# Longer bursts in a gated recurrence, and two gate products on split operands, in a two-layer hybrid attention trunk

## The chip, the cores and the metric

The kernel runs on one core of a Trainium2 chip. A core has a matrix engine (TensorE, "PE" in the profile, with its weight loads as "PEld"), a vector engine (VectorE, "DVE"), a scalar engine (ScalarE, "ACT"), GpSimd ("POOL") and a queue engine that issues the DMAs ("SP"). Matrix results land in PSUM, of which this kernel uses eight banks of 128 x 512 float32; everything else is in SBUF. The metric is the device time of one execution in microseconds (us); lower is better. Three runs of the kernel before took 2611.86, 2612.74 and 2614.28 us.

## What is computed

Two layers over 2048 tokens of width 1024. Each layer normalises and modulates its input, projects it, and sends the result through two branches: four heads of gated linear attention (GLA), and four heads of differential softmax attention. The change touches the GLA branch and one line on the way into the softmax branch. The reference, cut to the GLA branch:

```python
log_a = jax.nn.log_sigmoid((glr @ w_gk + b_gk)) / 16.0        # glr: tokens x 16, w_gk: 16 x 256
log_a = log_a.reshape(B, nc, 64, 4, 64)                       # chunks of 64 tokens, 4 heads, 64 wide
b = jnp.cumsum(log_a, axis=2)
b_end = b[:, :, -1]
k_dec = k * jnp.exp(b_end[:, :, None] - b)
u = jnp.einsum('bnchk,bnchv->nbhkv', k_dec, v)                # one 64 x 128 update a chunk and head
a = jnp.exp(b_end)
state = a_c[..., None] * state + u_c                          # scan over the 32 chunks
o = jnp.einsum('bnchk,nbhkv->bnchv', q, states)               # the chunk reads the state at its end
o = rms_norm(o, g_out) * silu(z)
```

## The kernel before

The sequence is cut into four units of 512 tokens (`u`), each of four tiles of 128 tokens (`t`), each of two chunks of 64. With two layers there are eight units. All large products are made of parts: an operand is split into a high part, rounded to the type `float32r`, and the low remainder, and three `float32r` products stand for one float32 product. Smaller products run on plain float32 operands; the trace shows such a matmul as two matmul instructions, a `float32r` one as a single one.

**What sets the order.** The program is first recorded, not issued. Six generators (projections, softmax heads, GLA, preparation of the next unit, modulation, query and key transposes) are interleaved by `run_streams` with their own estimates (`pe(cost, wait)`). The recorded operations then go through `Program.order` (lines 199 to 296), a list scheduler with a table of costs, latencies and free buffers, which fixes the sequence of each engine's queue. On the chip every engine works through its queue in that order and waits at the head of it. `prog.together` (line 160) makes a run of matmuls stay one burst on TensorE. All instructions are issued from line 305, so the profile's groups are told apart by the names of their tiles.

**The stages that the change touches.** In `gla_gen` (line 717), once a unit:

- The low-rank gate: 16 `float32r` matmuls of `wglr` with the input's high and low parts give `gps`, 32 rows of 512 tokens (16 rows for the weight's high part, 16 for its low part). VectorE copies them to `gT`, whose row 32 is set to 1.
- The gate's second product (line 742): four float32 matmuls, one for each tile of 128 tokens, of `gT` (33 rows) with `wgk` (33 rows x 256: the weight twice, and the bias). ScalarE and VectorE make the log-sigmoid `la` from it.
- The chunk sums (line 757): four float32 matmuls with the triangular matrix `tri`, 128 x 256 each; their exponential is `E`. Line 762 makes the chunks' totals from `la` and `chk`, 32 columns wide, in four column strips side by side (`a_sb` after a transpose).
- The recurrence (lines 805 to 849), for each tile of 128 tokens: a burst of 8 matmuls of 64 x 64 x 128 (`sc<-vN,E`) into two PSUM banks; four VectorE instructions that carry the state `Sn` over two chunks; a burst of 8 matmuls `po<-Sn,qT` into two other banks; the norm of the result: ScalarE squares (`sq`), VectorE sums (`gss`), GpSimd takes the power -1/2 (`gw`), VectorE multiplies into `osb` (shown under the tile's name `vN`).

The four PSUM banks of the tag `tp` serve these bursts and all of the gate's products, and also the softmax heads' scores (`sc`), transposes (`tp`) and outputs (`po`); the other four banks (`acc`) hold the large projections.

In `head_evac` (line 867), a softmax head's projection leaves PSUM: ScalarE copies queries and keys to `rw`, and VectorE writes the normalised ones to another tile, `qk`, which TensorE transposes later (`qk_gen`, line 892). `gate_weights` (line 444) loads `wgk` and splits the weight of the low-rank product into `wglr`; it runs in the start phase for layer 0 and during layer 0 for layer 1.

## Time and profile before

| | |
|---|---|
| runs, median of 3 | 2612.74 us (2611.86 to 2614.28) |
| the profiled execution | 2617.78 us, of which its span is 2616.0 us |
| granted TensorE clock, mean | 0.993 |
| DVE busy | 1758.4 us (67%) |
| ACT busy | 1202.3 us (46%) |
| POOL busy | 616.0 us (24%) |
| DMA | 476.12 MB, mean 182 GB/s |

The span runs from the first to the last instruction of one execution; the profiled execution was 5.04 us above the median of the runs. "Busy" is the time in which at least one instruction of the engine was in flight. Matmuls overlap: the next starts while the last still drains, so the mean duration of one (some 400 ns for 512 columns) is longer than the distance from one start to the next (some 230 ns), and it is the distance that costs time. In a timeline row, instructions that follow each other are merged with their count; its second column runs to the end of the last of them.

### The profile page before, as it was taken

What the parts mean: (1) busy time and instruction counts of PE and PEld (TensorE: products, weight loads), DVE (VectorE), ACT (ScalarE), POOL (GpSimd) and SP (SyncE); (2) the same over time, 40 slices, a digit from 0 to 9 for tenths busy, and PEclk for the clock granted to TensorE, in tenths of its full rate; (3) what the DMA queues carried; (4) which work ended last, traced back from release to release, by engine and by line L of the source; (5) the groups of instructions that cost most, each with busy time, mean ns of one, the idle gap of its engine ahead of it and who ended that gap; (6) DMA issues with size and microseconds to landing.
All of it is one profiled execution on the core that took longest, in us unless ns stands there. A gap on an engine that the chain in (4) does not pass through costs nothing. (4 is left out here: it accounts for less than half of the span.)

```text
span 2616.0 us, 40988 instructions
## 1 busy us (share of the span) xinstructions
PE 2513.0 (96%) x13987; PEld 2041.7 (78%) x13987; DVE 1758.4 (67%) x5072; ACT 1202.3 (46%) x2592; POOL 616.0 (24%) x820
## 2 busy tenths in 40 slices
PE   7999899999999999999999999999999999999997
PEld 4776677777888778888777777887788877888886
DVE  4778757874667846677748784657737786387864
ACT  3555523453354543544634564344614556154543
POOL 2445511122010210101144554111211111210111
PEclk9999999999999999999999999999999999999998
DMA  8777686555553455444267767554474443734342
GB/s 279 239 236 251 203 300 195 159 175 195 187 176 120 154 181 195 133 141 143 88 237 251 247 211 252 170 177 148 135 262 155 150 149 102 264 122 150 107 149 89
DMA packets 201612, 476.12 MB, mean 182 GB/s; under 512 B 20734, under 2 KB 78268, under 8 KB 201404
## 3 DMA queue, kind: packets, MB, share of 16 engines
q1 hardware_dynamic: 201404, 473.50, 54.2%
q8 instruction: 111, 1.82, 0.3%
q14 instruction: 97, 0.79, 0.1%
HBM read 362.29 MB, written 111.15 MB: 181 GB/s over the span
## 5 line engine op out<-in xcount | busy, mean ns | idle before, releaser
L305 PE MATMUL acc<-w,hhi 128*128 128x512 f32 x2560 | 838.9, 402 | 7.0 <-ACT ub L305 2.6
L305 PEld LDWEIGHTS acc<-w,hhi 128*128 128x128 f32 x2560 | 464.9, 189 | 100.5 <-ACT ub L305 7.7
L305 PE MATMUL acc<-w,hlo 128*128 128x512 f32 x1280 | 505.4, 396 | 0.0
L305 ACT ACTIVATE s<-s,mx 128x512 f32<-128x512 f32 (+15 forms) x256 | 308.1, 1204 | 351.0 <-DVE s L305 349.6
L305 PE MATMUL acc<-hhi,w 128*128 128x512 f32 x1024 | 370.7, 403 | 1.4 <-DVE z L305 1.2
L305 PE MATMUL acc<-w,oh 128*128 128x512 f32 x1024 | 330.8, 401 | 11.5 <-DVE t L305 7.1
L305 DVE TENSOR_SCALAR_CACHE_REDUCE s<-sc,mx 64x64 f32<-64x64 f32 (+5 forms) x640 | 307.1, 485 | 36.3 <-PE sc L305 19.1
L305 POOL MEMSET s<- 64x64 f32 x256 | 39.4, 156 | 1074.4 <-DVE s L305 527.1
L305 PEld LDWEIGHTS acc<-w,hlo 128*128 128x128 f32 x1280 | 241.4, 189 | 48.7 <-issue 1.3
L305 POOL TENSOR_TENSOR w<-raw,w 128x512 fp32r<-128x512 f32 x144 | 196.1, 1371 | 191.4 <-ACT w L305 158.9
L305 PEld LDWEIGHTS acc<-w,oh 128*128 128x128 f32 x1024 | 189.7, 190 | 58.4 <-DVE t L305 14.3
L305 PEld LDWEIGHTS acc<-hhi,w 128*128 128x128 f32 x1024 | 192.3, 188 | 39.2 <-PE tp L305 1.9
L305 PE MATMUL po<-Vj,aT 128*128 128x128 f32 x1536 | 206.1, 278 | 8.6 <-ACT aT L305 8.0
L305 ACT COPY aT<-tp 128x512 f32<-128x512 f32 (+2 forms) x320 | 162.2, 521 | 107.7 <-PE tp L305 104.4
L305 PEld LDWEIGHTS po<-Vj,aT 128*128 128x128 f32 x1536 | 191.6, 193 | 21.7 <-ACT aT L305 16.5
L305 DVE SCALAR_TENSOR_TENSOR s<-s,r 128x512 f32<-128x512 f32 (+2 forms) x320 | 200.2, 674 | 3.0
L305 PE MATMUL acc<-w,ol 128*128 128x512 f32 x512 | 201.2, 398 | 0.2
L305 PE MATMUL acc<-hlo,w 128*128 128x512 f32 x512 | 201.0, 393 | 0.0
L305 DVE TENSOR_SCALAR_CACHE_REDUCE s<-sc 128x512 f32<-128x512 f32 (+4 forms) x256 | 158.2, 622 | 57.6 <-PE sc L305 53.5
L305 DVE TENSOR_TENSOR ol<-oT,oh 128x512 fp32r<-128x512 f32 x128 | 104.7, 822 | 130.2 <-ACT oh L305 111.0
L305 PE MATMUL tp<-ident,s 128*128 128x128 f32 x1088 | 172.0, 275 | 13.5 <-DVE s L305 10.7
L305 PEld LDWEIGHTS tp<-ident,s 128*128 128x128 f32 x1088 | 130.5, 141 | 52.0 <-DVE s L305 11.9
(167 smaller groups left out, 4103.5 us busy)
## 6 DMA issues: line engine op xcount, KB each, us to landing
w<-wd SPq DMA_DIRECT2D x432, 512.0 KB, 3.7
wd<-w SPq DMA_DIRECT2D x144, 512.0 KB, 3.5
raw<-in_w_in_dram SPq DMA_DIRECT2D x112, 256.0 KB, 4.4
Kj<-kd SPq DMA_DIRECT2D x48, 512.0 KB, 4.7
wr<-in_w_ada_dram SPq DMA_DIRECT2D x128, 128.0 KB, 3.8
kd<-Kt SPq DMA_DIRECT2D x24, 512.0 KB, 3.4
Vj<-vd SPq DMA_DIRECT2D x48, 256.0 KB, 3.6
xt<-in_x_dram SPq DMA_DIRECT2D x16, 512.0 KB, 3.6
```

Source lines behind the costliest of these rows:

```text
L305: getattr(self.engines[e], method)(*[real(a) for a in args], **{k: real(v) for k, v in kw.items()})
```

## The change

Three parts, and two small ones. The diff below leaves out lines that only follow from these.

1. The recurrence works on 256 tokens at a time: bursts of 16 matmuls instead of 8, eight VectorE steps of the state between them, and the norm's instructions each twice as wide. The PSUM banks are filled in all 512 columns, before in 256. The state has six buffers instead of four.
2. The gate's second product is one `float32r` matmul a tile over 98 rows: `gT` holds the value's high part, its low part, its high part again and two rows of -1; `wgk` holds the weight's high part twice, its low part, and two rows that carry the bias with its sign turned. `gate_weights` prepares them with five VectorE instructions and one more DMA.
3. The chunk sums use `la` in a high and a low part (`lh`, `ll`), with a `float32r` copy of `tri`: two matmuls of 512 columns for two tiles, before two float32 matmuls of 256.
4. `head_evac` normalises `rw` in place, and the tile `qk` is gone; the tag `t2` of `p_t` has four buffers instead of three.

```diff
-    p_t = pool("p_t", 3)
+    p_t = pool("p_t", 4)
...
+    trir = cst.tile([P, P], F32R, name="trir")
+    V.tensor_copy(trir, tri)
...
     def gate_weights(l):
         y = layers[l]
-        y.wgk = cst.tile([33, 256], F32, tag="wgk", name=f"wgk{l}")
-        SY.dma_start(y.wgk[0:16, :], w_gk[l])
-        SY.dma_start(y.wgk[16:32, :], w_gk[l])
-        SY.dma_start(y.wgk[32:33, :], b_gk[l:l + 1, :])
+        wr = t2((34, 256))
+        for i in range(2):
+            SY.dma_start(wr[16 * i:16 * i + 16, :], w_gk[l])
+            SY.dma_start(wr[32 + i:33 + i, :], b_gk[l:l + 1, :])
+        y.wgk = cst.tile([98, 256], F32R, tag="wgk", name=f"wgk{l}")
+        V.tensor_copy(y.wgk[0:32, :], wr[0:32, :])
+        V.tensor_copy(y.wgk[32:64, :], wr[0:32, :])
+        V.tensor_tensor(y.wgk[64:96, :], wr[0:32, :], y.wgk[0:32, :].bitcast(F32), op=ALU.subtract)
+        wb = p_t.tile([34, 256], F32R, tag="sq", name="wb", bufs=2)
+        V.tensor_copy(wb[32:34, :], wr[32:34, :])
+        V.scalar_tensor_tensor(y.wgk[96:98, :], wb[32:34, :].bitcast(F32), keep[32:34, :], wr[32:34, :],
+                               op0=ALU.mult, op1=ALU.subtract)
...
-        gT = p_q.tile([33, 512], F32, tag="uT", name="gT", bufs=2)
-        V.memset(gT[32:33, :], 1.0)
+        gT = p_q.tile([98, 512], F32R, tag="uT", name="gT", bufs=2)
+        A.activation(gT[96:98, :], ones[96:98, 0:1].to_broadcast([2, 512]), AF.Copy, scale=-1.0)
         V.tensor_copy(gT[0:32, :], gps[0:32, :])
+        A.copy(gT[64:96, :], gps[0:32, :])
+        V.tensor_tensor(gT[32:64, :], gps[0:32, :], gT[0:32, :].bitcast(F32), op=ALU.subtract)
...
         for pr in range(2):
+            lap = la[:, 2 * pr:2 * pr + 2, :].rearrange("p a n -> p (a n)")
+            lh, ll = t2(dt=F32R), t2(dt=F32R)
+            A.copy(lh, lap)
+            V.tensor_tensor(ll, lap, lh.bitcast(F32), op=ALU.subtract)
             bp = sc()
-            for i in range(2):
-                t = 2 * pr + i
-                T.matmul(bp[:, i * 256:i * 256 + 256], tri, la[:, t, :], start=True, stop=True)
+            T.matmul(bp, trir, lh, start=True, stop=False)
+            T.matmul(bp, trir, ll, start=False, stop=True)
...
-        for t in range(TT):
+        for pr in range(TT // 2):
             ups = [sc() for _ in range(2)]
             first = len(prog.ops)
-            for pair in range(2):
-                for x_ in (0, 1):
...
+            for i in range(2):
+                t = 2 * pr + i
+                for pair in range(2):
+                    for x_ in range(2):
+                        for par in range(2):
...
+                            T.matmul(ups[par][half * 64:half * 64 + 64, c0:c0 + P], E[rs, t, hd * 64:hd * 64 + 64],
+                                     vN[rs, t, hd * P:(hd + 1) * P], start=True, stop=True)
             prog.together(first)
-            yield pe(0.65, 0.9)
+            yield pe(1.1, 0.9)
             Ss = []
-            for par in range(2):
-                cidx = 2 * t + par
-                Sn = p_sm.tile([P, 2, P], F32, tag="S", name="Sn", bufs=4)
+            for c in range(4):
+                i, par = c // 2, c % 2
+                Sn = p_sm.tile([P, 2, P], F32, tag="S", name="Sn", bufs=6)
                 for pair in range(2):
-                    V.scalar_tensor_tensor(Sn[:, pair, :], Sp[:, pair, :], a_sb[:, pair, cidx:cidx + 1],
-                                           ups[par][:, pair * P:pair * P + P], op0=ALU.mult, op1=ALU.add)
+                    c0 = i * 256 + pair * P
+                    V.scalar_tensor_tensor(Sn[:, pair, :], Sp[:, pair, :], a_sb[:, pair, 4 * pr + c:4 * pr + c + 1],
+                                           ups[par][:, c0:c0 + P], op0=ALU.mult, op1=ALU.add)
                 Sp = Sn
                 Ss.append(Sn)
-            yield pe(0, 2.0)
+            yield pe(0, 3.0)
...
+            for half in range(2):
+                sq = t2()
+                A.activation(sq, ops_[half], AF.Square)
+                V.tensor_reduce(ss[:, ts_, 2 * half:2 * half + 2], sq.rearrange("p (t a n) -> p t a n", t=2, a=2),
+                                axis=AX.X, op=ALU.add)
+            V.tensor_scalar(ss[:, ts_, :], ss[:, ts_, :], 1.0 / P, 4096.0 * EPS, op0=ALU.mult, op1=ALU.add)
+            G.tensor_tensor(wv[:, ts_, :].rearrange("p t a -> p (t a)"), ss[:, ts_, :].rearrange("p t a -> p (t a)"),
+                            mhalf[:, 0:8], op=ALU.pow)
...
-            n = p_q.tile([P, 256], F32, tag="qk", name="qk", bufs=4)
-            V.tensor_tensor(n.rearrange("p (a n) -> p a n", a=4), rw.rearrange("p (a n) -> p a n", a=4),
-                            rq[:, t, :].unsqueeze(2).to_broadcast([P, 4, 64]), op=ALU.mult)
-            qk.append(n)
+            rv = rw.rearrange("p (a n) -> p a n", a=4)
+            V.tensor_tensor(rv, rv, rq[:, t, :].unsqueeze(2).to_broadcast([P, 4, 64]), op=ALU.mult)
+            qk.append(rw)
```

The scheduler makes a new order of it. Three places matter to the prediction. In these rows `acc<-` are the large projections, `tp<-ident` transposes, `po<-Vj` and `po<-Vt` the softmax heads' outputs; `x8` is a run of eight.

TensorE, layer 0, second unit, first tiles of the recurrence, before:

```order
L305 MATMUL sc<-vN,E 64x128 x8
L305 MATMUL tp<-ident,s 128x128 x4
L305 MATMUL acc<-w,hlo 128x512
L305 MATMUL acc<-w,hhi 128x512 x2
L305 MATMUL acc<-w,hlo 128x512
L305 MATMUL tp<-ident,s 128x128 x4
L305 MATMUL po<-Vj,aT 128x128 x4
L305 MATMUL po<-Sn,qT 64x128 x8
L305 MATMUL po<-Vt,aT 128x128 x4
```

The same place in the changed kernel:

```order
L305 MATMUL sc<-vN,E 64x128 x16
L305 MATMUL tp<-ident,s 128x128 x4
L305 MATMUL acc<-w,hlo 128x512
L305 MATMUL acc<-w,hhi 128x512 x2
L305 MATMUL acc<-w,hlo 128x512
L305 MATMUL acc<-w,hhi 128x512
L305 MATMUL tp<-ident,s 128x128 x4
L305 MATMUL po<-Vj,aT 128x128 x4
L305 MATMUL po<-Sn,qT 64x128 x16
L305 MATMUL po<-Vt,aT 128x128 x4
```

The bursts are twice as long and half as many. Between the two of a round there is one projection matmul more than before.

TensorE, layer 0, third unit, the chunk sums (`tri`, now `trir`) and the chunks' totals (`chk`), before:

```order
L305 MATMUL acc<-w,ol 128x512
L305 MATMUL acc<-w,oh 128x512 x2
L305 MATMUL sc<-la,tri 128x256 x4
L305 MATMUL tp<-la,chk 32x256 x4
L305 MATMUL acc<-w,ol 128x512
```

And in the changed kernel:

```order
L305 MATMUL tp<-la,chk 32x256 x2
L305 MATMUL sc<-t_6719,trir 128x512
L305 MATMUL tp<-la,chk 32x256 x2
L305 MATMUL acc<-w,ol 128x512
L305 MATMUL sc<-t_6725,trir 128x512
L305 MATMUL sc<-t_6730,trir 128x512
L305 MATMUL acc<-w,ol 128x512
L305 MATMUL acc<-w,oh 128x512
L305 MATMUL sc<-t_6737,trir 128x512
```

The totals, which need `la` alone, now go first, and a chunk-sum matmul cuts their run of four in two. That is so in five of the eight units; in the other three the run stays whole.

VectorE, start phase, from the last of the small scalars (`nlam`) to the low-rank gate, before:

```order
L305 TENSOR_REDUCE l_632<-t_579 128x2
L305 CAST wglr_634<-t_609 128x8x16
L305 TENSOR_TENSOR nlam_639<-l_632 128x1
L305 TENSOR_TENSOR wglr_634<-t_609,wglr_634 128x8x16
L305 TENSOR_SCALAR nlam_639<-nlam_639 128x1
L305 COPY gT<-sc 32x512
```

And in the changed kernel:

```order
L305 TENSOR_REDUCE l_630<-t_578 128x2
L305 TENSOR_TENSOR nlam_635<-l_630 128x1
L305 TENSOR_SCALAR nlam_635<-nlam_635 128x1
L305 CAST wgk_640<-t_595 32x256 x2
L305 TENSOR_TENSOR wgk_640<-t_595,wgk_640 32x256
L305 CAST wb<-t_595 2x256
L305 SCALAR_TENSOR_TENSOR wgk_640<-wb,keep,t_595 2x256
L305 CAST wglr_653<-t_628 128x8x16
L305 TENSOR_TENSOR wglr_653<-t_628,wglr_653 128x8x16
L305 CAST gT<-sc 32x512
L305 TENSOR_TENSOR gT<-sc,gT 32x512
```

The five instructions that prepare `wgk` now stand ahead of the two that make `wglr`.

More of the change, by code (lines that the diff above doesn't have):

```diff
@@ L845, in gla_gen @@
-            for i in range(2):
-                V.tensor_tensor(osb[:, t, :].rearrange("p (a b n) -> p b a n", b=2, n=P)[:, i],
-                                ops_[i][:, 0:256].rearrange("p (a n) -> p a n", n=P),
-                                wv[:, t, 2 * i:2 * i + 2].unsqueeze(2).to_broadcast([P, 2, P]), op=ALU.mult)
+            for i in range(2):
+                for pair in range(2):
+                    for x_ in range(2):
+                        for half in range(2):
+                            par = x_ ^ half
+                            hs, q0, c0 = slice(half * 64, half * 64 + 64), (4 * pr + 2 * i + par) * CH, i * 256 + pair * P
+                            T.matmul(ops_[half][par * CH:par * CH + CH, c0:c0 + P], qT[hs, pair, q0:q0 + CH],
+                                     Ss[2 * i + par][hs, pair, :], start=True, stop=True)
@@ new lines, in gla_gen @@
+            prog.together(first)
+            yield pe(1.1, 0.5)
+            ts_ = slice(2 * pr, 2 * pr + 2)
+            for half in range(2):
+                sq = t2()
[3 more added lines that the diff above has]
+            V.tensor_scalar(ss[:, ts_, :], ss[:, ts_, :], 1.0 / P, 4096.0 * EPS, op0=ALU.mult, op1=ALU.add)
@@ new lines, in gla_gen @@
+            G.tensor_tensor(wv[:, ts_, :].rearrange("p t a -> p (t a)"), ss[:, ts_, :].rearrange("p t a -> p (t a)"),
+                            mhalf[:, 0:8], op=ALU.pow)
+            for half in range(2):
+                V.tensor_tensor(osb[:, ts_, :].rearrange("p t (a b n) -> p b t a n", b=2, n=P)[:, half],
+                                ops_[half].rearrange("p (t a n) -> p t a n", t=2, a=2),
+                                wv[:, ts_, 2 * half:2 * half + 2].unsqueeze(3).to_broadcast([P, 2, 2, P]), op=ALU.mult)
```

28 lines of the change are left out of this document (7 added, 21 removed).

## The prediction, made before the changed kernel ran

> **What bounds the kernel now.** I read the page's first line, then the stretches of the span, then who made TensorE wait, and last its timeline at each place that the diff touches.
>
> ```profile
> PE 2513.0 (96%) x13987; PEld 2041.7 (78%) x13987; DVE 1758.4 (67%) x5072; ACT 1202.3 (46%) x2592; POOL 616.0 (24%) x820
> ```
>
> ```profile
> core 0: us, PE busy (x) PEld busy (x) DVE busy (x) ACT busy (x) POOL busy (x), PEclk, DMA share, GB/s
> 0.00:65.00 65.00, 45.81 (x290) 29.30 (x291) 28.42 (x104) 20.85 (x41) 15.54 (x25) 0.97 0.85 278
> 650.00:980.00 330.00, 326.94 (x1858) 269.58 (x1857) 219.29 (x650) 151.24 (x313) 53.28 (x84) 1.00 0.50 164
> 1420.00:1600.00 180.00, 168.31 (x925) 130.99 (x924) 133.96 (x375) 105.62 (x259) 92.60 (x104) 0.99 0.66 226
> 2260.00:2550.00 290.00, 289.77 (x1715) 244.95 (x1713) 209.93 (x616) 133.56 (x261) 37.12 (x64) 1.00 0.44 144
> ```
>
> PE is busy for 2513 of 2616 us. Of the idle 103 us, 19 lie in the first 65 us; in the middle of a layer PE idles 3 of 330 us and 0.2 of 290, at the start of layer 1 it idles 12 of 180. Every other engine has a third of its time free. So PE's queue is the bound: a piece cut from it shortens the span by its own length, unless a new wait takes its place. The largest cause of PE's waits is small:
>
> ```profile
> PE po L305 <- ACT aT L305: 12.7, 21, 3.2
> ```
>
> Since busy PE is not PE at its peak, I price each edit by distances between starts.
>
> **The gate's second product.** It stands once in each of the eight units, 64 instructions in all; the rows below it are for the bursts:
>
> ```profile
> L305 PE MATMUL sc<-wgk,gT 33*128 33x256 f32 x64 | 15.9, 389 | 0.0
> L305 PE MATMUL sc<-vN,E 64*64 64x128 f32 x512 | 22.8, 282 | 0.9 <-DVE vN L305 0.5 <-DVE s L305 0.2
> L305 PE MATMUL po<-Sn,qT 64*64 64x128 f32 x512 | 21.7, 282 | 0.0
> ```
>
> ```profile
> 63.30 1.07 PE L305 MATMUL acc<-w,hhi 128*128 128x512 f32 x4
> 64.30 1.99 PE L305 MATMUL sc<-wgk,gT 33*128 33x256 f32 x8
> 66.22 0.50 PE L305 MATMUL acc<-w,hhi 128*128 128x512 f32 x1
> 66.56 0.40 PE L305 MATMUL acc<-w,hlo 128*128 128x512 f32 x1
> ```
>
> A 512-column `float32r` matmul takes 0.23 us from start to start (in the next fence from 305.32 to 305.55). Four of them from 63.30 end at 64.22; the product starts at 64.30, so 0.08 is lost on the way in. It holds PE to 66.22, 1.92. The projection behind it takes 0.34, 0.11 too much. Together 2.11 us a unit. Afterwards there are four `float32r` matmuls of 256 columns; the nearest rows are these:
>
> ```profile
> 383.05 0.28 PE L305 MATMUL sc<-Kt,qh 128*128 128x256 f32 x1
> 383.17 0.27 PE L305 MATMUL sc<-Kt,ql 128*128 128x256 f32 x1
> 383.28 0.40 PE L305 MATMUL acc<-hhi,w 128*128 128x512 f32 x1
> ```
>
> They are 0.115 apart with nothing lost around them: 0.46 for four, a gain of 1.65, eight times **13.2 us**. No row shows 98 rows. One bound is that the loss of 0.19 stays (11.7 us), the other this value; I take it, since shape of the columns and type agree. The Trainium skill (TensorEngine Tiling (Array Packing), Tiling Modes and Key Properties) lists row tiles of 64 and 32 and nothing between 64 and 128, and says that a change of mode drains TensorE: 33 rows would then be in a tiled mode and 98 in the whole array, which gives 13.2; the other reading gives 11.7. The 0.08 before the 33-row product agrees with it.
>
> **The chunk sums.** The third unit:
>
> ```profile
> 305.32 0.39 PE L305 MATMUL acc<-w,oh 128*128 128x512 f32 x1
> 305.55 1.89 PE L305 MATMUL sc<-la,tri 128*128 128x256 f32 x8
> 307.37 0.64 PE L305 MATMUL tp<-la,chk 128*32 128x256 f32 x8
> 307.94 0.50 PE L305 MATMUL acc<-w,oh 128*128 128x512 f32 x1
> 308.27 0.39 PE L305 MATMUL acc<-w,ol 128*128 128x512 f32 x1
> ```
>
> `tri` costs 1.82 including the step into `chk`; the four matmuls that replace it cost 0.92, and the step into `chk` (0.09, as into a burst below) stays. Gain 0.81, eight times **6.5 us**. The order cuts `chk` in two in five units. A run of `chk` takes 0.57 for four products side by side, its projection behind it 0.33 (0.10 too much). A second run costs between half of that run and all of it, with 0.19 on both sides: 0.48 to 0.76. I take the high end, since the four ran at the same time and not one after another: five times 0.76, **-3.8 us** (at least -2.4).
>
> **The bursts.** One burst in its place, and the same one cut off after 4, 8 and 12 instructions by the end of the window:
>
> ```profile
> 192.01 0.39 PE L305 MATMUL acc<-w,hlo 128*128 128x512 f32 x1
> 192.33 0.67 PE L305 MATMUL po<-Sn,qT 64*64 64x128 f32 x16
> 192.93 0.73 PE L305 MATMUL acc<-w,hhi 128*128 128x512 f32 x2
> 193.50 0.39 PE L305 MATMUL acc<-w,hlo 128*128 128x512 f32 x1
> ...
> 192.33 0.34 PE L305 MATMUL po<-Sn,qT 64*64 64x128 f32 x4
> 192.33 0.45 PE L305 MATMUL po<-Sn,qT 64*64 64x128 f32 x8
> 192.33 0.56 PE L305 MATMUL po<-Sn,qT 64*64 64x128 f32 x12
> ```
>
> Before it 0.09 is lost (0.32 for 0.23), it takes 0.60, and the two projections after it take 0.57 for 0.46: 0.80 us a burst. Each further four instructions add 0.11, so 32 take 0.60 + 0.44 = 1.04, and with the losses 1.24. Two old bursts cost 1.60: a gain of 0.36. The two groups of 512 instructions are 64 bursts; 32 of them go: **11.5 us**. If only the 0.20 around a burst is saved, 6.4.
>
> **The start.** PE waits once for the last of VectorE's small work:
>
> ```profile
> 58.04 0.39 PE L305 MATMUL sc<-hhi,wglr 128*32 128x512 f32 x1 [2.25 <-DVE nlam L305]
> ...
> 57.12 0.22 DVE L305 CAST wglr<-t 128x128 fp32r<-128x128 f32 x1
> 57.53 0.16 DVE L305 TENSOR_TENSOR nlam<-l 128x1 f32<-128x1 f32 x1 [0.20 <-ACT l L305]
> 57.61 0.29 DVE L305 TENSOR_TENSOR wglr<-t,wglr 128x128 fp32r<-128x128 f32 x1
> 57.81 0.15 DVE L305 TENSOR_SCALAR nlam<-nlam 128x1 f32<-128x1 f32 x1
> ```
>
> `wglr` is ready at 57.90. In the new order `nlam` ends first, at 57.96, then five preparations of `wgk`, between 0.15 and 0.29 each like the rows above (1.1 together), then `wglr`'s two, 0.5: 59.5. That is **-1.6 us**, at worst -3 when the one added DMA is late too, at best 0 when the small vectors land earlier. Layer 1's set lies in the middle of layer 0, under projections.
>
> **Edits at nothing.** The rows that price them:
>
> ```profile
> L305 ACT CAST w<-raw 128x512 fp32r<-128x512 f32 x144 | 88.8, 624 | 89.0 <-PE acc L305 43.7 <-DMA raw<-in_w_in_dram 26.7 <-DMA raw<-in_w_out_dram 5.2
> L305 DVE TENSOR_TENSOR ol<-oT,oh 128x512 fp32r<-128x512 f32 x128 | 104.7, 822 | 130.2 <-ACT oh L305 111.0 <-PE acc L305 18.8
> L305 DVE SCALAR_TENSOR_TENSOR Sn<-Sn,a_sb,sc 128x128 f32<-128x128 f32 x124 | 37.3, 342 | 5.1 <-PE sc L305 4.5
> L305 POOL TENSOR_TENSOR gw<-gss,mhalf 128x4 f32<-128x4 f32 x32 | 32.5, 1016 | 82.1 <-DVE gss L305 48.4 <-DVE r L305 16.5 <-DVE xss L305 16.1
> ```
>
> The splits add, in each unit, two casts (0.62) and two subtractions (0.82) for `la`, and some 0.6 each on ACT (a copy and the constant rows) and DVE (one subtraction) for `gT`; the wider norm gives part back in fewer instructions. That is some 2.5 us a unit on ACT and DVE, behind PE as long as projections stand between the gate's steps, which the order provides. Without that cover a unit's gate is about 2 us later, 16 us in all. In `head_evac`, the next head's copies into `rw` now wait for this head's transposes; 96 projection matmuls (22 us) lie between two heads, so nothing.
>
> **The sum.** 13.2 + 6.5 - 3.8 + 11.5 - 1.6 = 25.8 us less. Against the profiled execution, 2617.8 becomes 2592.0; the runs' median lies 5.04 us lower, so I predict 2612.7 - 25.8 = **2587 us**.
>
> **Rivals.** *The gain stops halfway.* The long bursts save only the 0.20 around them (6.4), 98 rows keep their loss (11.7), and the split waits some 0.5 us a unit (-4): 6.4 + 11.7 + 2.7 - 1.6 - 4 = 15, 2597 us or, with a little more waiting, up to 2602. For it: `PE po <- ACT aT` shows that a tight chain makes PE wait 0.6 us at a time. Against it: the growth of 0.11 for four is measured.
>
> *Banks held too long, slower.* A round of the recurrence now holds its two banks of the pool of four for longer: four more state steps (0.342 each, 1.4) ahead of the results, and a norm with a power of 8 columns instead of 4 (up to 1.0 more on POOL) and wider DVE work. The softmax heads' scores and transposes need the same banks, and PE waits in order. At 3 us in each of the 16 rounds it costs 48 us: 2635. It decides from 1.9 us a round on (31 us, the gain and 0.2%). For it: in 1420 to 1600, of these stretches the one where DVE is busiest, PE already idles. Against it: there are half as many rounds, and the new order leaves PE about as much other work between the bursts of a round. The Trainium skill (TensorEngine Tiling (Array Packing), PSUM Bottleneck) warns that packed matmuls speed up TensorE and not the emptying of PSUM; no row here shows a bank as a cause of waiting.
>
> *The waits shrink as well.* Half as many rounds also halve the handovers; if a sixth of the 84 us that PE idles after the first 65 us goes too, 14 us, it is 2573.
>
> *Nothing.* The saved PE time comes back as waits for DVE and ACT: 2613. Against it stand 289.77 of 290 us.
>
> **Chances.** The forecast 0.68, halfway 0.14, shrinking waits 0.08, slower 0.07, nothing 0.03. A difference under 0.2% (5 us) cannot be told from none here. Faster 0.90, within 0.2% 0.04 (nothing, and a slow case that nearly cancels), slower 0.06. The range reaches from the third rival to just past the halfway case: 2570 to 2604.
>
> **What would show it.** The gate's product at four instructions 0.115 apart with no gap before it; `trir` 0.23 apart; bursts of 32 lasting 1.04 with 0.09 ahead; PE busy some 26 us less and its idle time still near 103; PE's first `wglr` matmul near 59.6. I am wrong if PE idles 20 us more, with `sc` or `po` of the recurrence, or a score behind them, as what it waits for.

## The result: 0.2% slower, where 1% faster was predicted

The changed kernel takes 2619.78 us (median of 19 runs, 2612.75 to 2623.82), the kernel before in the same comparison 2614.28 us (19 runs, 2611.27 to 2618.48). The ratio is 1.0021, its 95% interval 1.0013 to 1.0028. The forecast was 2587 us, its range 2570 to 2604: the time lies outside, on the slow side. One run of a later experiment took 3511.48 us at a mean clock of 0.656, where that kernel's others had 0.994 or more; it is left out of its median.

The first line of the profile after: busy us, share of the span, instructions.

```profile
PE 2495.5 (95%) x13923; PEld 2031.5 (78%) x13923; DVE 1771.3 (68%) x5021; ACT 1215.3 (46%) x2592; POOL 608.3 (23%) x804
```

The span is 2620.5 us (before 2616.0). PE is busy for 17.5 us less than before, and idle for 125.0 us in place of 103.0. So work did go from TensorE, and more than its whole amount came back as waiting. The same four stretches as before (length, then busy us of PE, PEld, DVE, ACT and POOL, then the granted clock of TensorE):

```profile
0.00:65.00 65.00, 44.42 (x288) 28.13 (x289) 29.29 (x110) 20.93 (x42) 14.98 (x24) 0.95 0.87 283
650.00:980.00 330.00, 324.98 (x1847) 268.96 (x1846) 223.70 (x647) 151.80 (x313) 52.22 (x82) 0.99 0.49 164
1420.00:1600.00 180.00, 169.92 (x936) 132.17 (x936) 138.12 (x376) 109.62 (x263) 93.04 (x103) 0.99 0.67 229
2260.00:2550.00 290.00, 287.05 (x1702) 242.80 (x1701) 206.76 (x600) 132.72 (x256) 36.40 (x62) 1.00 0.42 144
```

PE's idle time grew from 19.2 to 20.6 us in the first row, from 3.1 to 5.0 in the second and from 0.2 to 3.0 in the last; in the third, where the rival of the held banks had looked for a loss, it fell from 11.7 to 10.1. The gain is not handed back in one place; the waits by who ended them (total us, times, longest) show several:

```profile
PE po L305 <- ACT aT L305: 16.1, 19, 3.2
PE tp L305 <- DVE s L305: 12.7, 24, 1.2
...
PE sc L305 <- DVE gT L305: 3.1, 8, 0.7
PE sc L305 <- DVE wglr L305: 3.1, 1, 3.1
```

The first was 12.7 us before and the second 11.4, the two of `gT` and `wglr` are new, and `nlam`'s 2.2 us went. Now the edited places themselves, in TensorE's timeline of the changed kernel. The gate's second product in the second unit:

```profile
304.27 0.39 PE L305 MATMUL acc<-w,oh 128*128 128x512 f32 x1
304.93 0.71 PE L305 MATMUL sc<-wgk,gT 98*128 98x256 f32 x4 [0.28 <-DVE gT L305]
305.48 0.40 PE L305 MATMUL acc<-w,oh 128*128 128x512 f32 x1
```

The product takes 0.55 instead of 1.92 us, and nothing is lost behind it. But it starts 0.66 us after the last projection, where 0.23 is the usual distance, because it waits for `gT`. The chunk sums of the next unit, `chk` now ahead of `trir`:

```profile
612.81 0.63 PE L305 MATMUL tp<-la,chk 128*32 128x256 f32 x4
613.37 0.50 PE L305 MATMUL sc<-t,trir 128*128 128x512 f32 x1
613.80 0.63 PE L305 MATMUL tp<-la,chk 128*32 128x256 f32 x4
614.36 0.50 PE L305 MATMUL acc<-w,ol 128*128 128x512 f32 x1
614.70 0.63 PE L305 MATMUL sc<-t,trir 128*128 128x512 f32 x2
```

Each half of `chk` holds PE for 0.56 us, as long as the whole run did before (0.57), and the matmul behind each half loses again. A burst of the recurrence:

```profile
195.01 0.39 PE L305 MATMUL acc<-w,hlo 128*128 128x512 f32 x1
195.33 1.10 PE L305 MATMUL po<-Sn,qT 64*64 64x128 f32 x32
196.36 0.74 PE L305 MATMUL acc<-w,hhi 128*128 128x512 f32 x2
```

It is 1.03 us long with 0.09 lost ahead of it and 0.12 behind (0.58 for two projections), 1.24 us in all, as the prediction had it. Last the start, where the projection of the gate's low-rank input waits for `wglr`:

```profile
57.56 0.60 PE L305 MATMUL sc<-hhi,wglr 128*32 128x512 f32 x1 [3.08 <-DVE wglr L305]
...
63.08 0.57 PE L305 MATMUL sc<-hlo,wglr 128*32 128x512 f32 x1
63.49 0.40 PE L305 MATMUL sc<-hhi,wglr 128*32 128x512 f32 x1
63.72 0.39 PE L305 MATMUL sc<-hlo,wglr 128*32 128x512 f32 x1
...
66.20 0.73 PE L305 MATMUL sc<-wgk,gT 98*128 98x256 f32 x4 [0.73 <-DVE gT L305]
```

After the wait of 3.08 us the matmuls stand 0.41 to 0.43 us apart until 63.49, and 0.23 from there on: TensorE runs at half its clock for that time. That turned out to matter in the whole kernel.

### The profile page after: what moved, and what is told of

Its sections match the earlier page's. It is cut to its first block, busy times and chain, and to the rows that moved or that the text cites. A ratio compares the mean times of both kernels' runs of the same rounds, so it can differ in the third digit from the quotient of the medians.

```text
span 2620.5 us, 40701 instructions
## 1 busy us (share of the span) xinstructions
PE 2495.5 (95%) x13923; PEld 2031.5 (78%) x13923; DVE 1771.3 (68%) x5021; ACT 1215.3 (46%) x2592; POOL 608.3 (23%) x804
## 4 chain that ended last, share of the span: by engine, by line
PE 71%; DVE 17%; DMA 3%; ACT 3%; issue 3%; POOL 1%; SPq 1%; DVEq 0%; ACTq 0%; POOLq 0%
PE acc L305 46%; PE sc L305 10%; PE po L305 8%; PE tp L305 7%; DVE s L305 6%; DVE t L305 3%; DMA wr<-in_w_ada_dram 1%; ACT s L305 1%; SPq L305 1%; DVE ql L305 1%; DVE am L305 1%; DVE hhi L305 1%; DMA w<-wd 1%; DVE r L305 1%; DVE hlo L305 1%
## 5 line engine op out<-in xcount | busy, mean ns | idle before, releaser
L305 PE MATMUL tp<-ident,s 128*128 128x128 f32 x1088 | 171.8, 275 | 16.9 <-DVE s L305 11.6
L305 POOL TENSOR_TENSOR rq<-qss,mhalf 128x4 f32<-128x4 f32 x128 | 129.8, 1032 | 215.4 <-DVE qss L305 215.3
```

Source lines behind the costliest of these rows:

```text
L305: getattr(self.engines[e], method)(*[real(a) for a in args], **{k: real(v) for k, v in kw.items()})
```

## The experiments

Eighteen kernels ran. The ratios are to the kernel before in the same comparison, whose median lay between 2612.9 and 2614.3 us; "idle" is the profiled span less PE's busy time. Span, busy and idle time and clock are of one profiled execution, which can lie some 4 us off the median (that of S took 2595.93 us, its fastest). S stands for the two small parts, described below.

| kernel | median us | ratio (95%) | span | PE busy | idle | clock |
|---|---|---|---|---|---|---|
| before | 2614.3 | | 2616.0 | 2513.0 | 103.0 | 0.993 |
| the change | 2619.8 | 1.0021 (1.0013-1.0028) | 2620.5 | 2495.5 | 125.0 | 0.992 |
| before's order, less PE work | 2601.4 | 0.9955 (0.9942-0.9967) | 2599.7 | 2495.9 | 103.8 | 0.993 |
| the change, more PE work | 2628.5 | 1.0062 (1.0050-1.0074) | 2628.5 | 2510.6 | 117.9 | 0.993 |
| before, order shaken | 2610.5 | 0.9994 (0.9983-1.0005) | 2609.6 | 2508.1 | 101.5 | 0.995 |
| the change, order shaken | 2612.4 | 0.9997 (0.9986-1.0007) | 2612.9 | 2491.8 | 121.1 | 0.993 |
| S: small parts | 2600.3 | 0.9947 (0.9933-0.9960) | 2594.2 | 2504.5 | 89.7 | 0.997 |
| S with three buffers | 2614.1 | 0.9997 (0.9988-1.0006) | 2609.9 | 2510.6 | 99.3 | 0.995 |
| S, order shaken | 2597.4 | 0.9938 (0.9925-0.9950) | 2599.7 | 2502.3 | 97.4 | 0.994 |
| S + 98 rows | 2600.0 | 0.9948 (0.9935-0.9960) | 2600.8 | 2500.7 | 100.1 | 0.996 |
| S + 98 rows, wglr first | 2597.1 | 0.9935 (0.9923-0.9947) | 2597.6 | 2501.3 | 96.3 | 0.994 |
| S + chunk split | 2607.9 | 0.9977 (0.9968-0.9986) | 2603.9 | 2511.2 | 92.7 | 0.994 |
| S + 98 rows + chunk split | 2611.7 | 0.9990 (0.9981-0.9998) | 2610.9 | 2503.8 | 107.1 | 0.993 |
| S + bursts | 2616.2 | 1.0004 (0.9995-1.0013) | 2613.9 | 2507.6 | 106.3 | 0.991 |
| S + bursts, squares in vN | 2615.1 | 1.0001 (0.9991-1.0011) | 2616.8 | 2510.5 | 106.3 | 0.991 |
| S + bursts, spaced 7 and 8 | 2606.2 | 0.9976 (0.9967-0.9985) | 2603.9 | 2498.3 | 105.6 | 0.995 |
| S + bursts, spaced 4 and 4 | 2600.5 | 0.9951 (0.9937-0.9964) | 2599.9 | 2496.0 | 103.9 | 0.995 |
| the change, spaced 4 and 4 | 2611.5 | 0.9993 (0.9982-1.0005) | 2610.7 | 2494.7 | 116.0 | 0.991 |
| the same, wglr first | 2607.0 | 0.9980 (0.9972-0.9989) | 2608.3 | 2493.5 | 114.8 | 0.990 |
| the same, no chunk split | 2602.4 | 0.9962 (0.9949-0.9975) | 2603.9 | 2496.3 | 107.6 | 0.991 |

### Is TensorE the bound at all?

Theory A: TensorE is the bound, its saving was real, and the new order of the queues lost it. B: TensorE's queue is not the bound that the prediction took it for. C: the rounds of 256 tokens make it wait. The first kernel keeps before's order of matmuls and gives the gate's product and the chunk sums one `float32r` matmul each; the low parts are left out of both. The lines that keep the planner from seeing this, so that its order stays, are not shown.

```diff
-        y.wgk = cst.tile([33, 256], F32, tag="wgk", name=f"wgk{l}")
+        y.wgk = cst.tile([33, 256], F32R, tag="wgk", name=f"wgk{l}")
...
-                T.matmul(bp[:, i * 256:i * 256 + 256], tri, la[:, t, :], start=True, stop=True)
+                T.matmul(bp[:, i * 256:i * 256 + 256], trir, la[:, t, :], start=True, stop=True)
```

> The kernel before with its own order on every engine, instruction by instruction; only the gate's second product and the chunk sums run as one float32r matmul each instead of two float32 instructions (their low parts are left out, so the output is slightly off). By the rows of before that takes 1.46 us a unit from TensorE at the gate's product and 1.27 at the chunk sums, 22 us in all. Theory A (TensorE is the bound, and what the change saved was lost by the new order of the instructions): 18 to 22 us faster than before, 2592 to 2597. Theory B (TensorE is not the bound; waits for VectorE and ScalarE fill whatever it saves): within 6 us of before, 2608 to 2616. Theory C (the rounds of 256 tokens themselves wait, for their PSUM banks or their state): as A, 18 to 22 us faster, since no round is changed here.

Measured: 2601.4 us, 11.5 less by the medians, 16.3 less by the profiled spans. PE's busy time fell by 17.1 us and its idle time grew by 0.8. In before's order a cut from TensorE's queue is passed on, two thirds of it by the medians and nearly all by the one profiled pair. The median lies between the ranges of A and B. The second kernel is the change with each matmul of the gate's product issued five times.

```diff
-            getattr(self.engines[e], method)(*[real(a) for a in args], **{k: real(v) for k, v in kw.items()})
+            n = 5 if e == "T" and method == "matmul" and args[1].buf.name == "gT" else 1
+            for _ in range(n):
+                getattr(self.engines[e], method)(*[real(a) for a in args], **{k: real(v) for k, v in kw.items()})
```

> The changed kernel in its own order, with each of the 32 matmuls of the gate's second product issued five times in a row (the same result each time): 16 more matmuls of 0.115 us a unit, 14.7 us more TensorE time, no other instruction added or moved. A: 11 to 15 us slower than the changed kernel, 2630 to 2635. B: within 4 us of it, 2616 to 2624. C: as A.

Measured: 8.8 us more by the medians, 10.7 by the ratios, again between A and B. PE's busy time grew by 15.1 us and 7.1 us of waiting vanished. So 58 to 71% of the added work counts in the change's order, and 67 to 69% of the work that was cut in before's (11.5 by the medians, 11.8 by the ratio, of 17.1). The two orders do not differ here by more than the noise: in both, TensorE's work counts by about two thirds. That makes a saving smaller; it does not turn it into a loss.

### Is it the luck of one order?

One price in the planner's table, the fixed cost of a VectorE operation, is raised from 68 to 78 ns, in both kernels. Nothing else differs.

```diff
-        return (0.52 if fast else 1.042) * n + 68 + 61 * scalars
+        return (0.52 if fast else 1.042) * n + 78 + 61 * scalars
```

> The kernel before with one constant of the scheduler's cost table moved (a VectorE instruction's fixed part from 68 to 78 ns), so the same instructions in a slightly other order. A: the order of before is an unusually good one, so 8 to 30 us slower, 2622 to 2644. B and C: within 5 us of before, 2609 to 2619.

> The changed kernel with the same constant moved. A: its TensorE work is 26 us less than that of e3, so 15 to 35 us faster than e3; against the changed kernel anywhere from 15 faster to 10 slower. B: within 6 us of e3 and of the changed kernel. C: within 6 us of the changed kernel (the rounds wait in any order), and not faster than e3.

Measured: before's ratio stays at 1 (0.9994, the interval holds 1), the change's falls from 1.0021 to 0.9997, some 6 us. So an order alone can be worth as much as the whole difference in the result. But with either order the change waits for some 20 us more than before (121.1 and 125.0 us idle, against 101.5 and 103.0), so its waiting is not one unlucky order. A falls here: it had the shaken kernel before at 2622 us or more, and the shaken change 15 to 35 us below it.

### The parts one at a time

S is the kernel before with two things that the prediction priced at nothing: the fourth scratch buffer (`p_t`, from which `t2` takes its tiles) and the query and key normalised in place. The other three add parts of the change to S. H blames the in-place write, G the gate's longer chain, R the rounds of 256 tokens.

```diff
-    p_t = pool("p_t", 3)
+    p_t = pool("p_t", 4)
...
-            n = p_q.tile([P, 256], F32, tag="qk", name="qk", bufs=4)
-            V.tensor_tensor(n.rearrange("p (a n) -> p a n", a=4), rw.rearrange("p (a n) -> p a n", a=4),
-                            rq[:, t, :].unsqueeze(2).to_broadcast([P, 4, 64]), op=ALU.mult)
-            qk.append(n)
+            rv = rw.rearrange("p (a n) -> p a n", a=4)
+            V.tensor_tensor(rv, rv, rq[:, t, :].unsqueeze(2).to_broadcast([P, 4, 64]), op=ALU.mult)
+            qk.append(rw)
```

> The kernel before with the two small parts alone: queries and keys normalised in place (no tile qk), four buffers for t2. No TensorE work changes. Theory H (the in-place write holds rw until TensorE has transposed it, and ScalarE's next copies out of PSUM wait): 8 to 25 us slower than before. Theories G (the longer chain of the gate makes TensorE wait) and R (the rounds of 256 tokens make it wait): within 6 us of before.

> f1 with the recurrence in rounds of 256 tokens (16 matmuls a burst, six state buffers), the gate as before. The bursts save TensorE 11.5 us. R: the rounds give all of it back, so between 2 faster and 12 slower than f1. G: 7 to 12 us faster than f1. H: as G against f1, but slower than before.

> f1 with both gate products on split operands (98 rows, and the chunk sums in two parts), the recurrence in rounds of 128 tokens as before. The products save TensorE 13.2 + 6.5 - 3.8 = 16 us. G: the chain from the low-rank gate to E, later by a subtraction at each split, gives it back: between 3 faster and 10 slower than f1. R: 10 to 16 us faster than f1.

> f1 with the second product over 98 rows alone, the chunk sums in float32 as before. It saves TensorE 13.2 us and loses 1.6 at the start. G: if the product's own split is the late link, no faster than f1 (within 4 us); if it is the split of the log gates, 8 to 12 us faster than f1 and faster than f3. R: 8 to 12 us faster than f1.

Measured: S alone gains 14.0 us, which none of the three had. On top of it the 98 rows change nothing (2600.0), the two gate parts together cost 11.4, and the bursts cost 16.0. G and R hold in their signs, H falls. The change holds a large gain that had no price and losses where gains had been forecast. They do not simply add: 16.0 + 11.4 - 14.0 would make it 13.4 us slower than the kernel before, and it is 5.5 slower, so the parts share some of their losses.

### Where the gain of S comes from, and two tests on the parts

Theory T: the fourth buffer is the gain, and the wide squares and the halves `lh` and `ll` use it up. U: the round itself makes TensorE wait. O: the luck of an order.

```diff
-                sq = t2()
+                sq = vN[:, 2 * pr + half, :]
```

> The kernel before with the in-place q and k alone (the next head's normalisation written over rw, the qk buffers gone); the pool of scratch tiles t2 stays at three buffers. Theory T: the fourth scratch buffer made the 14 us of the small parts, and the long bursts' wide squares and the chunk split's lh and ll use it up; then this is 2610 to 2617. Theory O: the gain is the luck of an order of the queues; then anything from 2598 to 2617, with the four-buffer kernel under a shaken order (the run f1_p1 below) back at 2606 or more. If the in-place write itself is the gain: 2597 to 2604.

> The small parts and the long bursts (2616 when run so), with the squares of the norm written into the dead rows of vN and no longer into a scratch tile. Theory T: the wide squares hold the scratch buffers that the projections and the softmax heads need; without that the bursts give what PE saves, 2590 to 2602. Theory U, the round of 256 tokens itself (banks held, one long chain in place of two short ones, fewer places for other work) makes PE wait: still 2611 to 2618. Theory O: 2600 to 2617, with no place in the trace that explains it.

> The small parts (in-place q and k, four scratch buffers; 2600) under a slightly shaken order: the planner's fixed price of a VectorE operation is 78 ns in place of 68. Theory T and the in-place reading: the gain is a resource and stays, 2597 to 2604. Theory O: it is the luck of one order, 2606 to 2615.

> The small parts and the chunk sums from high and low parts, without the 98 rows. If the split itself loses (lh and ll take two of four scratch buffers twice a unit and two more steps stand in the gate's chain): 2607 to 2614, as the difference of 11.7 between the two kernels with and without it. If the loss needs both gate parts (the second layer's wgk preparations stand ahead of the out-projection's copies on VectorE near 950 us): 2594 to 2602. By PE's work alone it would be 2597.

Measured: with three buffers the gain is gone (2614.1), and TensorE's queue is then the same row for row as before's. With four and a shaken order it stays (2597.4). So the fourth scratch buffer, on top of the in-place write, makes the 14 us. The buffer alone did not run, and whether it acts through the order that the planner makes with it, or while the kernel runs, was not separated. The squares in `vN` leave the bursts at 2615.1: T falls for them. The chunk split alone costs 7.6 us.

### The order or the round?

P says that the places in the queue decide, U the round. The same bursts run with other distances between the steps of a round, which only the planner reads (the first row after the state steps, the second after the norm; here 4.0 and 4.0, in the other kernel 7.0 and 8.0). The kernel before had 2.0 and 3.0 for each 128 tokens, 10 us for 256; the change gives 256 tokens 6 us.

```diff
-            yield pe(0, 3.0)
+            yield pe(0, 4.0)
...
-            yield pe(0, 3.0)
+            yield pe(0, 4.0)
```

> The small parts and the long bursts (2616), with the distances written into the round for the planner changed: 7.0 instead of 3.0 us of TensorE's time after the state steps and 8.0 instead of 3.0 after the norm. Nothing is computed otherwise. Counted in the order of TensorE's queue, the work in stretches of over 2 us without a projection is 123 us for the small parts alone, 151 with the bursts, 135 here. Theory P, the places decide: each us of it costs about a us (28 us more bare work, 27 us lost against PE's saving), so 2616 - 16 = 2600, between 2596 and 2606. Theory U, the round itself costs: 2611 to 2618 whatever the places.

> The same with 4.0 and 4.0 us. The bare work in the order is 139 us, and the last stretch of the program is as short as with the small parts alone (17 us of work instead of 18). Theory P: 2616 - 12 = 2604, between 2599 and 2609. Theory U: 2611 to 2618.

> The small parts and the 98 rows (2600.0), with wglr loaded and prepared ahead of wgk. If the start's loss (137 to 140 us for the first 384 projections but the start, where 1.7 us less were due) comes of wglr standing behind wgk: some 5 us less, 2593 to 2597, and PE's first wglr matmul about 2 us earlier. If wgk's own four loads and five preparations then make the gate's second product wait as long: 2598 to 2602.

Measured: 2606.2 and 2600.5 us, 10.0 and 15.7 less than the same bursts at the old distances (7 and 14 by the ratios). Both leave U's range of 2611 to 2618, so the old order cost that much. That is shown of the order, not of these distances: the shake alone gave the changed kernel some 6 us. The count of bare work (work without a projection matmul beside it) by which the two were forecast ranked them the wrong way round, so it is no measure to plan by. The first lines of three profiles: S, then the bursts, then the bursts spaced 4 and 4.

```profile
PE 2504.5 (97%) x13987; PEld 2036.8 (79%) x13987; DVE 1756.6 (68%) x5072; ACT 1201.6 (46%) x2592; POOL 615.4 (24%) x820
```

```profile
PE 2507.6 (96%) x13987; PEld 2048.1 (78%) x13987; DVE 1761.4 (67%) x4992; ACT 1197.1 (46%) x2560; POOL 608.5 (23%) x804
```

```profile
PE 2496.0 (96%) x13987; PEld 2041.6 (79%) x13987; DVE 1752.4 (67%) x4992; ACT 1200.6 (46%) x2560; POOL 608.9 (23%) x804
```

From the second to the third the same matmuls are busy for 11.6 us less, and the idle time hardly changes (106.3 to 103.9). What changed between these two executions is the clock, 0.991 to 0.995 in the mean. In steps of 3.4 us the clock is 1.00 or 0.50, so 0.009 x 2 x 2613.9 = 47 us ran at half clock, and 26 us with the new spacing (in S 16). Executions of one kernel differ in this: the mean clock over all of them is 0.9921 with the bursts, 0.9950 at 4 and 4 and 0.9958 in S, by the same working 41, 26 and 22 us. At most half of such time is lost, so the clock makes at most 8 of the 14.7 us between the first two kernels' mean times (2615.4 and 2600.7), and the rest was not traced. One place to see it is the last bare stretch, from the last projection of the last unit to the next one. It holds the final softmax heads and nothing else. S, the bursts, the bursts spaced 4 and 4:

```profile
2525.30:2560.60 35.30, 26.17 (x168) 21.36 (x167) 18.71 (x57) 16.64 (x29) 1.77 (x4) 0.94 0.05 16
```

```profile
2537.90:2580.10 42.20, 30.70 (x176) 25.01 (x174) 20.74 (x63) 17.22 (x31) 2.31 (x5) 0.87 0.04 13
```

```profile
2529.70:2567.50 37.80, 26.43 (x170) 21.84 (x168) 19.54 (x59) 16.86 (x29) 1.77 (x4) 0.95 0.04 15
```

Eight more matmul instructions than in S are left for it with the bursts, which is 1 to 2 us of work; it takes 6.9 us longer, at a clock of 0.87. In the changed kernel the same stretch is 41.9 us long, in the kernel before 35.3. How a wait becomes slow work is seen at 1838 us of the kernel with the bursts, in steps of 3.4 us:

```profile
1835.20:1838.60 3.40, 3.34 (x22) 2.70 (x21) 3.10 (x15) 1.59 (x5) 0.54 (x1) 1.00 0.24 58
1838.60:1842.00 3.40, 1.45 (x11) 1.22 (x12) 2.91 (x9) 3.40 (x8) 0.29 (x1) 1.00 0.28 101
1842.00:1845.40 3.40, 3.40 (x15) 2.92 (x13) 2.58 (x5) 1.98 (x6) 2.54 (x3) 0.50 0.00 0
1845.40:1848.80 3.40, 3.37 (x18) 2.31 (x18) 3.35 (x7) 2.66 (x7) 3.38 (x4) 1.00 0.00 0
```

```profile
1840.96 1.16 PE L305 MATMUL po<-Vj,aT 128*128 128x128 f32 x8 [1.94 <-ACT aT L305]
```

One wait of 1.94 us for a softmax head's probabilities leaves PE busy for 1.45 of 3.40 us, and the next 3.40 us, full of work, run at 0.50. Some 1.7 us are lost after the wait is over.

The order does not explain all. The waits for the softmax heads grew with the bursts and stayed with the better spacing: in S, with the bursts, and with them at 4 and 4:

```profile
PE po L305 <- ACT aT L305: 10.6, 15, 3.2
PE tp L305 <- DVE s L305: 8.6, 16, 1.5
```

```profile
PE po L305 <- ACT aT L305: 16.2, 19, 3.5
PE tp L305 <- DVE s L305: 12.8, 24, 1.2
```

```profile
PE po L305 <- ACT aT L305: 16.5, 18, 3.5
PE tp L305 <- DVE s L305: 12.8, 25, 1.2
```

So the bursts save TensorE 0.36 us each by their rows, some 11 us, and add 14 to 17 us of waiting to the profile of S in all three spacings (idle 89.7 to 103.9, 105.6, 106.3). At the best spacing they come to nothing (2600.5 against 2600.3). These two waits together tell all twenty profiles apart: 24.8 to 32.3 us in the ten kernels with long bursts, 16.1 to 24.1 in the ten without, whatever the order.

For the start, the third kernel moves `wglr` ahead of `wgk` on SP's queue and on VectorE.

```diff
+        y.wglr = cst.tile([P, KT, 32], F32R, tag="wglr", name=f"wglr{l}")
+        gr = t2((P, KT, 16))
+        SY.dma_start(gr, w_in[l, :, C_GLR:C_GLR + 16].rearrange("(k p) n -> p k n", p=P))
...
         wr = t2((34, 256))
```

With the 98 rows as they are, and with `wglr` first:

```profile
57.64 0.61 PE L305 MATMUL sc<-hhi,wglr 128*32 128x512 f32 x1 [3.13 <-DVE wglr L305]
...
64.82 0.75 PE L305 MATMUL sc<-wgk,gT 98*128 98x256 f32 x4 [0.71 <-DVE gT L305]
```

```profile
55.55 0.40 PE L305 MATMUL sc<-hhi,wglr 128*32 128x512 f32 x1 [1.04 <-DVE nlam L305]
...
61.51 0.73 PE L305 MATMUL sc<-wgk,gT 98*128 98x256 f32 x4 [2.09 <-DVE gT L305]
63.69 2.50 PE L305 MATMUL acc<-w,hhi 128*128 128x512 f32 x5 [1.45 <-ACT w L305]
```

The product comes 3.3 us earlier and the kernel takes 2597.1 us, 2.8 less, though the intervals of the two ratios overlap. As the expectation allowed, part of the gain turns into a wait for `gT`, 2.09 us. Another 1.45 us go for ScalarE's `w`, and the projections behind it run at half clock. After 384 matmuls of the large projections the profile is 2.0 us ahead (162.5 us instead of 164.5).

### The whole change, mended

> The whole change (2619.8), with 4.0 instead of 3.0 us as the distances after the state steps and after the norm. Bare work in the order 138 us instead of 151. Theory P: as the long bursts alone gained 15.7 from these distances, 2604, between 2600 and 2610. If the three parts hinder each other whatever the places: 2612 to 2620.

> The run before it, with wglr loaded and prepared ahead of wgk. With the 98 rows alone that was worth 2.8 us; it also moves wgk's preparations behind wglr's in the middle of layer 0. Theory: 1 to 5 us below the run before it, 2599 to 2605; by PE's work alone nothing.

> The run before it without the split of the chunk sums: the small parts, the 98 rows with wglr first, and the bursts at 4.0 and 4.0. If the split costs as it did before (7.6 to 11.7): 2590 to 2597, the fastest of all. If its cost was the places too: 2598 to 2605. By PE's work alone it would be 2.7 slower than the run before it.

Measured: 2611.5, 2607.0 and 2602.4 us: 8.3, 4.5 and 4.6 less, one after another. Each step goes the forecast way, but the first two times lie above their ranges. The first gains half of what the bursts alone did, and its clock stays at 0.991. The third lands in the range of the other reading: in the new order the split costs less. With all mended the change still isn't faster than S alone. The fastest kernels are S with a shaken order (2597.4) and S with the 98 rows and `wglr` first (2597.1), both about 0.6% under the kernel before.

## Why the prediction was wrong

**The premise.** "A piece cut from it shortens the span by its own length, unless a new wait takes its place" held to about two thirds: 11.5 us of 17.1 in before's order, 8.8 to 10.7 of 15.1 in the change's. That alone would have left two thirds of the forecast gain. What turned the gain into a loss stands behind the "unless": the sum has no term for a new wait. I read full stretches (289.77 of 290 us) as proof that the whole queue was tight. Those stretches stayed nearly full (287.05), but PE's idle time grew in many other places, most in 1600 to 1930 (4.8 to 11.6 us; the rows are before's and the change's) and 980 to 1300 (3.6 to 8.0).

```profile
1600.00:1930.00 330.00, 325.23 (x1747) 264.22 (x1747) 197.02 (x582) 135.91 (x309) 70.64 (x98) 1.00 0.55 187
1600.00:1930.00 330.00, 318.40 (x1721) 259.43 (x1720) 193.11 (x571) 136.72 (x307) 69.50 (x95) 1.00 0.55 187
```

**The bursts, +11.5 forecast, the step that failed most.** The size on TensorE was right (1.03 us a burst, 0.09 ahead). The failed step is that no wait was set against it, on the ground that the new order "leaves PE about as much other work between the bursts of a round". That work was there, but it was not what mattered: the softmax heads' outputs and transposes waited longer, and with the waits came half clock. Measured, the bursts cost 16.0 us, 27 worse than forecast. Of these, 14 to 16 are the order, shown by changing it alone; up to 8 of them are the clock. The rest is waiting that no order tried removed. Which step of the round makes those heads wait was not settled. The rival *Banks held too long* had the right sign, but its 3 us in each round would stay with any spacing, and 14 of the 16 us did not. Whether held banks make up the waiting that stayed was not tried.

**The gate's second product, 13.2.** The spacing of 0.115 came for two of the three steps (0.115 to 0.127); the first takes 0.19 to 0.22, so four hold PE for 0.55 and not 0.46. Nothing is lost behind them. The step "nothing lost around them" failed ahead of the product. Start to start with its neighbours, a steady unit takes 0.73 + 0.55 + 0.24 us, before 0.32 + 1.92 + 0.34: 1.06 us saved and not 1.65, in all eight units 7.9. Of the difference 0.50 is the wait for `gT`, which all eight units show, and 0.09 the first step. Where `gT` is ready, as in one unit of S with the 98 rows at 1280 us, the product starts 0.27 behind its neighbour. So pricing the splits "at nothing" was wrong for `gT`: the product stands too close behind its inputs in the queue. The runs gave nothing in sum for the 98 rows (2600.0 against 2600.3). In the profiled pair the start is 5.6 us later after 384 projections, which is most of what the product saves; that this is the whole reason is not shown.

**The chunk sums, 6.5 - 3.8.** The rows that the prediction calls the third unit (305 us) are the second's; all units have the same ones, so the sum stays. `trir` is 0.23 apart as forecast in the five units that have `chk` cut, and 0.3 to 0.8 in the others. The mis-sized term is the cut of `chk`. I took 0.76 us a cut. In the five units that have it cut, the rows at 612 give 0.32 + 0.56 + 0.43 + 0.56 with the steps into both halves, before 0.31 + 0.57: 0.99 a cut. In the other three `chk` waits for `la` or has other neighbours, and in all it takes 15.5 us with the steps into it, before 7.1: 8.4 lost, not 3.8. Against `trir`'s gain, TensorE saves nothing by this part, and the split adds two casts and two subtractions a unit. Alone it cost 7.6 us, on top of the 98 rows 11.7, and 4.6 was gained by leaving it out of the mended change. One place where the two gate parts collide is VectorE's queue in the last unit of layer 0 in the changed kernel:

```profile
949.73 0.59 DVE L305 CAST wgk<-t 32x256 fp32r<-32x256 f32 x2
950.36 0.42 DVE L305 TENSOR_TENSOR wgk<-t,wgk 32x256 fp32r<-32x256 f32 x1
950.80 0.28 DVE L305 CAST wb<-t 2x256 fp32r<-2x256 f32 x1
951.12 0.23 DVE L305 CAST wglr<-t 128x128 fp32r<-128x128 f32 x1
951.38 0.48 DVE L305 SCALAR_TENSOR_TENSOR wgk<-wb,keep,t 2x256 fp32r<-2x256 f32 x1
951.88 0.29 DVE L305 TENSOR_TENSOR wglr<-t,wglr 128x128 fp32r<-128x128 f32 x1
952.09 1.28 DVE L305 TENSOR_TENSOR t<-acc,gate 128x512 f32<-128x512 f32 x2
```

```profile
952.83 0.73 PE L305 MATMUL acc<-w,oh 128*128 128x512 f32 x2 [2.00 <-DVE t L305]
```

The next layer's weights stand ahead of the copy that empties the projections' banks, and PE waits for 2.00 us. The prediction had put this set "under projections" at no cost. The rest of the split's cost was not traced to a step.

**The start, -1.6.** The direction was right, the size against the kernel before too (the product at 66.20 instead of 64.30 us, 1.9), with some luck, since before's own start ran at half clock from 59.0 to 62.4; but not the place: the first `wglr` matmul came at 57.56 and not near 59.6, and the loss came afterwards, at half clock. Against S, whose product starts at 60.04 and whose start ran at full clock, the loss is over 6 us. These are single executions; the clock of the start differs between them.

**What was not priced.** The fourth scratch buffer stands in the diff's first line, and no term has it. With the in-place write it is worth 14 us, more than any gain that was forecast, and makes up for half of the 27.4 us that the other parts lost one by one.

**The tests named in the prediction.** The bursts and `trir` came as said, the product with a gap before it, PE's busy time fell by 17.5 instead of 26, and "I am wrong if PE idles 20 us more" came true with 22, though spread over many waits: 4.7 us of it stand at the heads' outputs and transposes (28.8 instead of 24.1), 3.1 at `gT`, and only 0.7 at the recurrence's own `Sn`. The rival *Nothing*, at 2613 and a chance of 0.03, was the nearest; slower than before had 0.06.

## What to carry to other kernels

Where a planner orders the queues, a change of the code is a change of the order, and here the order was worth as much as the work: price the parts one at a time, and shake the order once to see how much of a difference is its luck. Look for the stretches without filler work, such as the last one here: a wait there can cost twice, by itself and by the clock behind it. Buffer counts are part of a diff: give each a term of its own.

## What the hardware showed that was not expected

TensorE's clock reacts to waits of some 2 us. In the profiled execution of the kernel with the bursts eleven stretches of 3.4 to 6.8 us run at 0.50, each right behind a step of 3.4 us in which PE was busy for 13 to 59% of the time, as at 1838.60 above; the last of them lies behind TensorE's last matmul and costs nothing. The twenty profiles, cut at the clock's own steps from 40 us on, say it more sharply. Of the steps at full clock, all 136 in which PE was busy for under 43% were followed by half clock, 28 of 138 between 43 and 60%, and 3 of 14548 above that, these three at the start, near 60 us.

The Trainium skill (TensorE: Matmul & The Clock Gate, HAM oscillation — how this bites in real kernels) gives as its rule that gaps of TensorE should stay under about 3.4 us. The trace is stricter than this rule: one wait of 1.94 us, with transposes and short matmuls on both sides, was followed by 3.40 us at half clock. The page's section What's actually happening has a window of 3413 ns and two states, 1.2 and 2.4 GHz, and the trace agrees in the lengths (3.41 and 6.83 us) and in the two states (0.50 and 1.00). The mean clock doesn't rank kernels by itself, though: the bursts alone and the mended change without the chunk split both have 0.992 over all their runs, and take 2616.2 and 2602.4 us.

A run of 2, 4 or 6 of the `chk` instructions, which work on 32 columns of the array each, takes 0.55 to 0.56 us at full clock and without a wait, a run of 8 takes 0.57. Cutting such a run in two doubles it.
